# New durations and new ranks for the planner that writes the instruction order of a decoder-layer kernel

## The chip, the cores and the metric

The kernel runs on one core of one Trainium2 chip. The core has a matrix engine (TensorE, PE in the profile; PEld is its weight load), a vector engine (VectorE, DVE), an activation engine (ScalarE, ACT), a general engine (GpSimd, POOL), and SyncE (SP), whose queue issues all the loads and stores here. The engines run side by side, each in the order of its own instruction list, and wait for one another by semaphores. The metric is the device time of one execution in microseconds (us). A profiled execution has a span, from its first instruction to its last; the device time holds the span and a little on both sides of it.

## The reference

The layer takes 1024 tokens of width 1024. In outline:

```python
mod = silu(c) @ w_ada + b_ada                 # shift, scale, gate
h = rms_norm(x, norm_w) * (1 + scale) + shift
u, g_pool, q, k, v, g_attn, qi, ki, wi = split(h @ w_in)
pool_out = pool_mixer(u, w_pool, pool_scale) * silu(g_pool)
q, k = rope(rms_norm(q)), rope(rms_norm(k));  qi, ki = rope(qi), rope(ki)
score = sum_over_8_index_heads(relu(qi . ki) * wi)      # causal
attn  = softmax attention of 8 query heads on 2 key heads,
        only on the 256 keys of the highest score       # per query
y = concat(pool_out, attn * silu(g_attn)) @ w_out
x = x + gate * y
```

`pool_mixer` takes means over the last 2, 4, 8 and 16 tokens minus the token itself, and multiplies them by a matrix per group. Ties in the score go to the earlier key.

## The kernel before

**Stages.** (1) Lead-in: tokens are loaded as rows (`xr`), normed, transposed on PE in pairs of 128 channels (`m<-c,xr`), copied from PSUM to SBUF as `xt` and scaled and shifted to `h`. The w_ada rows (`wa`) are reduced on DVE to scale and shift. (2) Projection: every fp32 product is made from two rounded parts, a high part (`hhi`, `wh`) and the rest (`hlo`, `wl`), in three matmuls: `hhi,wh`, `hhi,wl`, `hlo,wh`. Weights arrive as `ld` and are split by a cast (`wh`) and a subtraction (`wl`). (3) The index scores of the 8 query tiles of 128 tokens, and the search for each row's 256th best score by bisection on the 16-bit halves of the keys: tiles 5 to 7 on ACT (`ajunk<-key,xq`), tiles 2 to 4 on DVE (`junk<-key,xq`), each round followed by small updates (`aq`, `xq`, `yq`). (4) Attention by query tile: scores (`m<-kT,qr`), masked maxima on DVE (`ex<-m,key` or `ex<-m,mask`, and `mx`), exponentials on ACT (`ex<-ex,mx,c`), transposes (`m<-c,ex`), copies (`pw`), products with the values (`m<-pw,vrow`), gating (`mah`, `mal`). Before it, each query half is squared (`st`), split (`qsh`, `qsl`) and summed by head on PE (`m<-qsh,c`, `m<-qsl,c`) for the query norm. After the bisection, a running sum over a tile's ties (`selw<-selw`, a scan) leaves the first ones as the mask. (5) The pooling mixer: window sums on DVE (`nx`, `u`), `m<-u,c` on PE, gating (`gp`), split into `mph` and `mpl`. (6) The output projection in two halves, pooled (`m<-mph,wh` and so on) and attended (`m<-mah,wh`), each finished by a multiply-add (`xo`) and a store.

**What sets the order.** A planner inside the kernel writes all five instruction lists, once, while the kernel is built. Each stage is a set of strands (Python generators such as `token_out`, `queries`, `unit`, `finish`) that yield one operation at a time. `Flow.run` (line 393) asks the next operation of every strand for the time at which it could start by the planner's own clock, adds the strand's rank (`EARLY`; for PE `LAST`, and `SAFE` as a margin on data), and issues the one with the smallest sum. An operation's duration in that clock comes from `Op._cost` (line 169), and the time at which a transfer lands from `Op.issue` (line 224). `Either` (line 284) holds an operation that several engines can do; the engine is the one that would end first, with `FAVOUR` and the engine's backlog added. `KEEP`, `MIX`, `AHEAD`, `WA_AHEAD`, `IK`, `GM` and others limit how many buffers or PSUM banks a strand may take ahead of others, or how far one strand may run ahead of another.

All operations are emitted at one line, L240 of this kernel, so that the profile's rows differ by engine, operation and tile names alone. The lists further below give one engine's instructions in program order; there the scan is written as `SCALAR_TENSOR_TENSOR selw<-selw` and a masked maximum as `ISA ex,mx<-m,key` with an `ISA mx` that reads out its accumulator.

Of the kernel before, what the change touches and what calls it, by code (L numbers as in the profile page):

```python
# [36 lines left out]
ROOM = {"b": 36, "ld": 2, "st": 3, "wh": 4, "wl": 4, "kt": 2, "sg": 2, "selw": 1, "m": 8}  # L37


EARLY = {"main": 0.6, "fill": 0.4, "weights": 0.0, "evac": -1.0, "side": 0.2, "h": -0.2, "mods": -0.2,  # L40
         "select": -0.1, "scores": -0.6, "attend": -1.1, "late": 1.0, "kv": -0.3, "qi": -0.8, "pick": -0.6,
         "mix": -0.33, "rotated": 0.23, "query_loads": 0.21, "exps": -0.11, "score_sums": -1.07,
         "key_value_out": -0.93, "index_queries": -0.86, "norm": -0.46, "gate_loads": -1.94, "token_scales": -3.22,
         "gate_mods": -0.39, "unit": -1.06, "index_scores": -0.91, "lead_loads": 1.12, "out": -1.01,
         "lead_out": -0.62, "weight_loads": 0.77, "key_value_weights": -0.8, "main_line": 1.15, "output_line": 1.13,
         "turns": -1.46, "finish": -1.64, "index_keys": -1.47, "h_block": 0.28, "attention_keys": -0.36,
         "turned": -1.0, "h_blocks": -0.59, "gated": -2.15, "modulations": 0.89, "low": 0.65, "gear": 0.42,
         "attention": -0.86, "maxima": -0.99, "score_relus": -0.67, "gated 7": -1.82, "gated 3": -1.0,
# [5 lines left out]
         "exps 5": -0.25, "key_value_out 4": -3.2, "query_norms": 0.27, "exps 8": -0.52, "key_value_out 5": -1.22,  # L54
# [6 lines left out]
         "key_value_out 6": -2.24, "norm 1": -2.54, "gear 4": -1.05, "products": -1.29, "shift 4": -0.32,  # L61
         "norm 5": -1.64, "low 1": -2.52, "turns 6": -1.25, "gated 6": -2.43, "turns 8": -1.76, "h_block 3": -0.55,
         "shift": 0.73, "gear 8": -1.24, "lead_line": 1.29, "gear 7": -0.86, "index_queries 3": -3.25,
         "index_queries 1": -2.08, "lead_splits": -0.3, "shift 5": -0.34, "first_block": -2.64, "shift 2": -0.27,
         "lead_out 1": -0.38, "shift 8": 1.56, "out 7": -0.3, "unit 3": -1.17, "turns 3": -3.11,
         "key_value_out 1": -2.25, "exps 4": -0.27, "mix 2": -0.2, "exps 2": 0.46, "out 6": -0.73, "gated 8": -2.42,
         "out 5": -2.76, "token_turns": -1.26, "token_out 9": -0.19, "h_half 14": -0.44, "h_half 10": -0.92,
# [6 lines left out]
         "token_tile 4": -0.11, "token_out 10": -1.74, "token_out": -0.47, "token_out 14": -0.77,  # L74
         "token_out 13": -0.78, "token_out 5": -0.25, "h_half 7": -0.24, "token_tile 7": -0.74, "token_tile": -0.23}

SELECT = -0.425
LAST = {"main": 0.12, "fill": -0.081, "scores": 0.035, "attend": -0.104, "evac": -0.027, "qi": 0.257,
        "side": -0.376}

SAFE = {"side": 1.0, "unit": 0, "query_norms": 0.69, "h_block": 0.59, "rotated": 0.48, "query_loads": 0,
        "norm": 0.29, "weight_loads": 0.85, "key_value_out": 0.39, "turned": 0.26, "finish": 0, "index_keys": 0.85,
        "main_line": 0, "output_line": 0, "gate_mods": 1.06, "selection": 0, "low": 0.27, "maxima": 0,
        "attention": 0.44, "lead_out": 0, "score_relus": 0, "lead_loads": 0.28, "score_sums": 0.18, "mix": 0.96,
        "main": 0, "modulations": 0.09, "out": 0.39, "turns": 0.34, "exps": 0, "lead_line": 1.22, "shift": 0,
        "token_scales": 0.08, "index_scores": 0.19, "products": 0.3, "index_queries": 0.34, "attend": 0,
        "weight_splits": 0, "token_turns": 0, "gear": 0, "key_value_weights": 0.29}

COLD = 17.877

# [11 lines left out]

AGE = 0.37

PW_POOL = 0.101
XO_POOL = 0.117
BACK = 0.854
SPAN = 0.119

QK = 1  # L110
IK = 1
FK = 0
PK = 0

GM = 4

MIX = 5
KEEP = 7

FLY = 2  # L120

PV = 5

WA_AHEAD = 1
AHEAD = 4
XN_AHEAD = 2

FAVOUR = {"DVE": 0.245, "ACT": -0.111, "POOL": 0.27}
TABLES = {AF.Silu: 1, AF.Sqrt: 2, AF.Exp: 3}


# [6 lines left out]
class Op:  # L138
# [30 lines left out]
    def _cost(self, aps, kw):  # L169
        size = [a.free_size() for a in aps]  # L170
        n = max(size)
        eng = self.eng
        if eng == "SP":
            return 0.42
        if eng == "PE":
            rate = 2 if self.name == "transpose" else 4 if aps[1].dtype == F32 else 1
            if self.name == "transpose" and aps[1].shape[0] == 64:
                self.mode = "rows"
                return size[0] * 0.000417 + 0.007
            if self.name != "transpose" and min(aps[0].shape[0], aps[1].shape[0]) == 64:  # L180
                self.mode = "rows" if aps[1].shape[0] == 64 else "columns"
                return size[0] * 0.000417 * rate / 2 + 0.007
            return max(0.427 if rate == 4 else 0.109, size[0] * 0.000417 * rate + 0.0135)
        wide = [a for a, k in zip(aps, size) if k == n]
        psum = any(a.space == PSUM for a in wide)
        half = all(mybir.dt.size(a.dtype) == 2 for a in wide)
        if eng == "ACT":
            t = 0.000833 * n + (0.05 if psum else 0.094)
            t += 0.093 * sum(isinstance(kw.get(k), bass.AP) for k in ("scale", "bias", "accum_out"))
            return t  # L190
        if eng == "POOL":
            if self.name == "tensor_tensor":
# [31 lines left out]
    def issue(self, flow):  # L224
        t = self.start(flow)
# [15 lines left out]
        end = t + us  # L241
        flow.clock[self.eng] = end
        if self.eng == "SP":
            flow.dma = max(flow.dma, t + 1.8) + self.kw_bytes() / 4.0e5
            end = flow.dma + (0.35 if self.kw_bytes() > 1e5 else 2.0)
            flow.landed.append(end)
        for a in self.outs:
# [1401 lines left out]
```

## Time and profile before

| what | us |
|---|---|
| device time, median of 3 runs (510.72 to 511.76) | 511.74 |
| span of the profiled execution | 508.7 |
| median minus span | 3.0 |
| PE busy in the span | 481.7 (95%) |
| DVE busy | 420.0 (83%) |
| ACT busy | 380.8 (75%) |
| POOL busy | 148.8 (29%) |

The granted clock of TensorE was 0.995 of full speed on average. For the profiled execution the record gives the span and no device time of its own, so that it is set beside the median of the three runs. In a timeline row the columns are start, duration, engine, line, operation, out<-in tiles, shape and type, how many instructions the row merges, and in brackets the idle time of the engine just before the row and what ended it. By stretches of the span, PE is busy for 17.2 of the first 31.0 us, for 121.75 of the next 122.0, for 84.3 of 87.0 (153 to 240 us), 71.98 of 72.0 (to 312), 79.2 of 83.0 (to 395), 85.7 of 89.0 (to 484), and 21.5 of the last 25.

### The profile page before, as it was taken

Reading aid. Unit: us, or ns where it says so; the run is one execution under the profiler, and the core shown is the slowest. Engines: PE = TensorE matmul, PEld = TensorE weight load, DVE = VectorE, ACT = ScalarE, POOL = GpSimd, SP = SyncE. Lnnn points to the kernel's source line nnn. Section 1 sums busy time; section 2 is a strip of 40 time slices with the busy share of each in tenths; the row PEclk is TensorE's granted clock in tenths of the full one; section 3 lists DMA queues with packets and bytes.
Section 4 is the critical chain, followed back from the end, with each engine's and each line's share of the span. In section 5 each row is a group of like instructions: output and inputs, shape, how many; then the busy total and the mean of one; then the engine's idle time right before and its main releaser. Section 6 shows DMA issues by size and latency. Waiting matters only on the chain.

```text
span 508.7 us, 8547 instructions
## 1 busy us (share of the span) xinstructions
PE 481.7 (95%) x2924; PEld 362.3 (71%) x2924; DVE 420.0 (83%) x914; ACT 380.8 (75%) x877; POOL 148.8 (29%) x182
## 2 busy tenths in 40 slices
PE   1889999999999989999999998999998999999997
PEld 1668999767777867877887776786575558644486
DVE  4987798799789789999999999978889796667453
ACT  3896641687778999999935999899997766669410
POOL 3598053002001133546131235613531232400000
PEclk9999999999999999999999999999998999999999
DMA  8998513011105112111110112685542043521045
GB/s 298 410 407 298 170 41 125 21 36 51 62 22 186 43 42 84 41 42 43 42 52 33 42 43 79 208 273 157 171 128 65 23 124 97 193 63 43 1 150 182
DMA packets 28172, 58.36 MB, mean 115 GB/s; under 512 B 3808, under 2 KB 8416, under 8 KB 28128
## 3 DMA queue, kind: packets, MB, share of 16 engines
q1 hardware_dynamic: 28128, 57.81, 33.9%
q8 instruction: 23, 0.38, 0.3%
q14 instruction: 21, 0.17, 0.1%
HBM read 47.32 MB, written 10.49 MB: 114 GB/s over the span
## 4 chain that ended last, share of the span: by engine, by line
PE 73%; DVE 14%; DMA 6%; ACT 3%; issue 2%; POOL 0%; SPq 0%; DVEq 0%; POOLq 0%
PE m L240 73%; DVE junk L240 4%; DMA wa<-wada 4%; ACT ex L240 3%; DVE ex L240 3%; DVE sw L240 1%; DMA xr<-xR 1%; DVE selw L240 1%; DVE xq L240 1%; DMA ld<-wout 1%; DVE wa L240 1%; DVE mpl L240 0%; DVE qr L240 0%; DVE nx L240 0%; SPq L240 0%
## 5 line engine op out<-in xcount | busy, mean ns | idle before, releaser
L240 PE MATMUL m<-hhi,wh 128*128 128x512 f32 (+1 forms) x320 | 120.8, 400 | 0.6 <-ACT xt L240 0.3
L240 PE MATMUL m<-hhi,wl 128*128 128x512 f32 (+1 forms) x320 | 115.2, 383 | 0.0
L240 PE MATMUL m<-hlo,wh 128*128 128x512 f32 (+1 forms) x320 | 114.9, 382 | 0.0
L240 ACT ACTIVATE ajunk<-key,xq 128x768 bf16<-128x768 uint16 (+2 forms) x93 | 96.4, 1036 | 1.3
L240 PEld LDWEIGHTS m<-hhi,wh 128*128 128x128 f32 x320 | 59.1, 190 | 17.6 <-issue 4.0
L240 DVE TENSOR_SCALAR_CACHE_REDUCE junk<-key,xq 128x384 bf16<-128x384 uint16 (+2 forms) x93 | 69.0, 742 | 2.3 <-DVE xq L240 0.2
L240 POOL TENSOR_TENSOR wl<-ld,wh 128x512 fp32r<-128x512 f32 x42 | 58.2, 1390 | 38.0 <-DVE wh L240 16.7
L240 PEld LDWEIGHTS m<-hhi,wl 128*128 128x128 f32 x320 | 59.2, 190 | 12.2 <-issue 1.7
L240 PEld LDWEIGHTS m<-hlo,wh 128*128 128x128 f32 x320 | 58.7, 189 | 11.6
L240 ACT ACTIVATE ex<-ex,mx,c 128x384 f32<-128x384 f32 (+7 forms) x64 | 54.9, 860 | 6.6 <-DVE mx L240 4.3
L240 DVE SCALAR_TENSOR_TENSOR score<-kt,c,score 128x1024 f32<-128x1024 f32 (+5 forms) x42 | 40.7, 970 | 7.1 <-ACT kt L240 5.0
L240 ACT ACTIVATE kt<-m 128x512 f32<-128x512 f32 (+1 forms) x80 | 37.7, 525 | 11.0 <-DVE score L240 5.2
L240 ACT CAST wh<-ld 128x512 fp32r<-128x512 f32 x31 | 19.3, 624 | 30.5 <-issue 10.6
L240 PE MATMUL m<-kT,qr 64*128 64x512 f32 (+3 forms) x192 | 39.9, 516 | 1.0 <-DVE mx L240 1.0
L240 DVE SCALAR_TENSOR_TENSOR xo<-m,c,xo 128x512 f32<-128x512 f32 (+1 forms) x25 | 18.2, 729 | 24.2 <-PE m L240 16.9
L240 DVE CUSTOM_DVE_ANT_0 ex<-m,key 128x512 f32<-128x512 f32 (+1 forms) x48 | 30.8, 662 | 5.0 <-ACT ex L240 3.6
L240 PE MATMUL m<-pw,vrow 128*64 128x512 f32 x144 | 33.3, 605 | 0.0
L240 PEld LDWEIGHTS m<-kT,qr 64*128 64x128 f32 x192 | 20.4, 190 | 16.1 <-issue 10.6
L240 POOL TENSOR_SCALAR wh<-ld 128x512 fp32r<-128x512 f32 x26 | 17.0, 654 | 48.9 <-PE m L240 28.1
L240 ACT COPY pw<-m 128x512 f32<-128x512 f32 x51 | 26.5, 595 | 5.7 <-PE m L240 5.5
L240 PEld LDWEIGHTS m<-c,ex 64*128 64x128 f32 x576 | 21.0, 138 | 10.9 <-DVE mx L240 3.7
L240 PE MATMUL m<-c,ex 64*128 64x64 f32 x576 | 24.0, 227 | 3.8 <-DVE mx L240 1.8
(199 smaller groups left out, 1029.5 us busy)
## 6 DMA issues: line engine op xcount, KB each, us to landing
wa<-wada SPq DMA_DIRECT2D x24, 512.0 KB, 9.1
ld<-wet SPq DMA_DIRECT2D x16, 512.0 KB, 3.4
ld<-wout SPq DMA_DIRECT2D x24, 256.0 KB, 3.3
xr<-xR SPq DMA_DIRECT2D x8, 512.0 KB, 7.8
xo<-xT SPq DMA_DIRECT2D x16, 256.0 KB, 3.8
y_d<-xo SPq DMA_DIRECT2D x16, 256.0 KB, 2.4
xo<-y_d SPq DMA_DIRECT2D x15, 256.0 KB, 3.1
outT<-xo SPq DMA_DIRECT2D x15, 256.0 KB, 2.5
```

The source lines that it names most:

```text
L240: self.fn(*self.args, **self.kw)
```

## The change

No operation of the layer changes. The planner gets other numbers, and so writes other lists:

- the duration it assumes for a scan becomes twice as long per element, that of a 16-bit two-input operation on DVE half as long;
- a first transfer is assumed to take longer: 3.0e5 bytes per us up to 8 us instead of 4.0e5, and 0.35 us more for a small one;
- nearly all ranks (`EARLY`, `LAST`, `SAFE`) have new values, some strands get one of their own, and the limits, thresholds and engine preferences change.

```diff
-EARLY = {"main": 0.6, "fill": 0.4, "weights": 0.0, "evac": -1.0, "side": 0.2, "h": -0.2, "mods": -0.2,
+EARLY = {"main": 0.05, "fill": 0.4, "weights": 0.0, "evac": -1.0, "side": 0.2, "h": -0.13, "mods": -0.15,
...
-LAST = {"main": 0.12, "fill": -0.081, "scores": 0.035, "attend": -0.104, "evac": -0.027, "qi": 0.257,
-        "side": -0.376}
+LAST = {"main": 0.053, "fill": -0.081, "scores": -0.282, "attend": -0.169, "evac": 0.48, "qi": 0.124, "side": -0.652}
...
-PW_POOL = 0.101
-XO_POOL = 0.117
-BACK = 0.854
-SPAN = 0.119
+PW_POOL = 0.147
+XO_POOL = 0.11
+BACK = 0.835
+SPAN = 0.122
...
-IK = 1
+IK = 3
...
-GM = 4
+GM = 3
-MIX = 5
-KEEP = 7
+MIX = 4
+KEEP = 3
...
-WA_AHEAD = 1
-AHEAD = 4
+WA_AHEAD = 3
+AHEAD = 5
...
-FAVOUR = {"DVE": 0.245, "ACT": -0.111, "POOL": 0.27}
+FAVOUR = {"DVE": 0.278, "ACT": -0.348, "POOL": 0.273}
...
+        if self.name == "tensor_tensor_scan":
+            return 0.00212 * n + 0.069
+        if self.name == "tensor_tensor" and half:
+            return 0.00052 * n + 0.075
...
-            flow.dma = max(flow.dma, t + 1.8) + self.kw_bytes() / 4.0e5
+            flow.dma = max(flow.dma, t + 1.8)
+            flow.dma += self.kw_bytes() / (3.0e5 if flow.dma < 8 else 4.0e5) + (0.0 if self.kw_bytes() > 1e5 else 0.35)
```

The loads stand in the same order as before for the first 41 instructions of SP's list. PE's list has the same stages in the same order; what moves is where the shorter pieces stand between the long rows of projection matmuls, which engine takes some of the shared operations, and the order on DVE, ACT and POOL. Three places:

**The last query norm, on DVE** (`st_2091` before and `st_2100` after are the squares of the last half; the split `qsl` of it stood on POOL before, behind a weight split). Before:

```order
L240 TENSOR_SCALAR junk_2077,cq_330_2076<-key_82,xq_325_2056 128x384
L240 TENSOR_SCALAR junk_2079,cq_330_2076<-key_83,xq_325_2056 128x512
L240 CAST qsh_1964<-st_2091 128x512
L240 TENSOR_SCALAR junk_2084,cq_330_2076<-key_84,xq_325_2056 128x640
L240 TENSOR_SCALAR yq_341_2102<-xq_325_2056 128x3
L240 CAST wh_2092<-ld_1885 128x512
```

Now:

```order
L248 TENSOR_SCALAR junk_2066,cq_328_2065<-key_82,xq_324_2050 128x384
L248 TENSOR_SCALAR junk_2069,cq_328_2065<-key_83,xq_324_2050 128x512
L248 TENSOR_SCALAR junk_2085,cq_328_2065<-key_84,xq_324_2050 128x640
L248 CAST qsh_1970<-st_2100 128x512
L248 TENSOR_TENSOR qsl_1971<-st_2100,qsh_1970 128x512
L248 TENSOR_TENSOR aq_335_2088<-cq_328_2065,kcq_247_1761 128x3
```

The cast now stands behind the whole round of the bisection, and the subtraction follows it on the same engine. On PE the 12 norm matmuls that read these parts come after 1076 matmuls instead of 1064. Of the next group, `m<-u,c`, the first comes after 1226 matmuls instead of 1220, and the next 4 norm matmuls stand right behind it; two products `qr<-qr,cos` of the rotation between the two places have gone from DVE to POOL, and one sum `qr<-qr,sw` from POOL to DVE.

**The scan of the tile of 768 keys, on DVE,** among the masked maxima of the tile of 640 keys (`key_84`). Before:

```order
L240 ISA ex_4339,mx_4161<-m,key_84,mx_4161 128x128
L240 ISA mx_4161 128x1
L240 SCALAR_TENSOR_TENSOR selw_4343<-selw_4343 128x768
L240 ISA ex_4340,mx_4161<-m,key_84 128x512
L240 ISA mx_4161 128x1
L240 TENSOR_TENSOR gt_4160<-gt_4160,m 128x512
L240 ISA ex_4340,mx_4161<-m,key_84,mx_4161 128x128
```

Now:

```order
L248 ISA ex_4245,mx_4178<-m,key_84,mx_4178 128x128
L248 ISA mx_4178 128x1
L248 ISA ex_4227,mx_4051<-m,key_83 128x512
L248 ISA mx_4051 128x1
L248 SCALAR_TENSOR_TENSOR selw_4250<-selw_4250 128x768
L248 ISA ex_4280,mx_4178<-m,key_84 128x512
L248 ISA mx_4178 128x1
L248 TENSOR_TENSOR gt_4050<-gt_4050,m 128x512
```

Before, one head of the tile was still to come behind the scan; now four are. On PE the score matmuls of these heads (`m<-kT,qr`) stand in pairs between groups of 16 transposes and one group of 6 products with the values, before as now.

**The first copies of the lead-in, on ACT** (`xt_187` before and `xt_194` after hold the first two channel blocks). Before:

```order
L240 CAST wh_154<-ld_151 128x512
L240 CAST wh_208<-ld_151 128x512
L240 COPY xt_187<-m 128x8x64
L240 COPY xt_206<-m 128x8x64
L240 COPY xt_187<-m 128x8x64
L240 COPY xt_206<-m 128x8x64
```

Now:

```order
L248 CAST wh_154<-ld_151 128x512
L248 COPY xt_194<-m 128x8x64
L248 CAST wh_218<-ld_151 128x512
L248 COPY xt_214<-m 128x8x64 x2
L248 COPY xt_194<-m 128x8x64
L248 COPY xt_238<-m 128x8x64
```

The second half of the first block is now the fourth copy, where it was the third. Behind it, the `hlo` of the second block has moved from DVE to POOL, where it stands behind two scalings of `xr`.

More of the change, by code (lines that the diff above doesn't have):

```diff
@@ L37 @@
 ROOM = {"b": 36, "ld": 2, "st": 3, "wh": 4, "wl": 4, "kt": 2, "sg": 2, "selw": 1, "m": 8}
-EARLY = {"main": 0.6, "fill": 0.4, "weights": 0.0, "evac": -1.0, "side": 0.2, "h": -0.2, "mods": -0.2,
[L41 to L48, printed above, removed]
[5 rows of a table removed]
-         "exps 5": -0.25, "key_value_out 4": -3.2, "query_norms": 0.27, "exps 8": -0.52, "key_value_out 5": -1.22,
[6 rows of a table removed]
[L61 to L67, printed above, removed]
[6 rows of a table removed]
-         "token_tile 4": -0.11, "token_out 10": -1.74, "token_out": -0.47, "token_out 14": -0.77,
-         "token_out 13": -0.78, "token_out 5": -0.25, "h_half 7": -0.24, "token_tile 7": -0.74, "token_tile": -0.23}
@@ L77 @@
-SELECT = -0.425
-LAST = {"main": 0.12, "fill": -0.081, "scores": 0.035, "attend": -0.104, "evac": -0.027, "qi": 0.257,
-        "side": -0.376}
[L81 to L87, printed above, removed]
+EARLY = {"main": 0.05, "fill": 0.4, "weights": 0.0, "evac": -1.0, "side": 0.2, "h": -0.13, "mods": -0.15,
+         "select": -0.1, "scores": -0.6, "attend": -1.34, "late": 1.0, "kv": -0.68, "qi": -0.53, "pick": -0.6,
+         "mix": -0.01, "rotated": 0.38, "query_loads": -1.36, "exps": -0.18, "score_sums": -1.08,
+         "key_value_out": -1.28, "index_queries": 0.52, "norm": 0.72, "gate_loads": -5.55, "token_scales": -3.22,
+         "gate_mods": -0.39, "unit": -1.2, "index_scores": -3.29, "lead_loads": -1.01, "out": -0.59,
+         "lead_out": 0.68, "weight_loads": 0.13, "key_value_weights": -0.76, "main_line": 3.69, "output_line": 0.46,
+         "turns": 3.89, "finish": -1.64, "index_keys": -1.39, "h_block": -2.15, "attention_keys": -0.43,
+         "turned": -1.0, "h_blocks": -0.03, "gated": -3.43, "modulations": 1.22, "low": 0.65, "gear": 0.43,
+         "attention": -2.89, "maxima": -1.17, "score_relus": -0.67, "gated 7": -2.67, "gated 3": -0.53,
[5 rows of a table added]
+         "key_value_out 7": -2.65, "exps 5": -0.0, "key_value_out 4": -2.92, "query_norms": 1.0, "exps 8": -0.52,
[6 rows of a table added]
+         "shift 6": -0.04, "key_value_out 6": -3.9, "norm 1": -5.07, "gear 4": -1.05, "products": -2.42,
+         "shift 4": -1.67, "norm 5": -2.01, "low 1": -1.0, "turns 6": -7.13, "gated 6": -2.43, "turns 8": -1.76,
+         "h_block 3": -0.55, "shift": 0.73, "gear 8": -1.24, "lead_line": 0.74, "gear 7": -2.86,
+         "index_queries 3": -3.49, "index_queries 1": -2.08, "lead_splits": -0.3, "shift 5": -1.05,
+         "first_block": -2.64, "shift 2": -0.27, "lead_out 1": -0.76, "shift 8": 2.12, "out 7": -0.24,
+         "unit 3": -1.42, "turns 3": -4.24, "key_value_out 1": -2.25, "exps 4": -0.61, "mix 2": -0.2, "exps 2": 0.46,
+         "out 6": -0.48, "gated 8": -2.41, "out 5": -1.53, "token_turns": -1.26, "token_out 9": -0.03,
[6 rows of a table added]
+         "token_tile 8": -0.49, "h_half 13": -0.21, "token_tile 4": -0.11, "token_out 10": -1.62, "token_out": 1.8,
+         "token_out 14": -1.63, "token_out 13": -1.31, "token_out 5": -0.25, "h_half 7": -0.24,
+         "token_tile 7": -0.74, "token_tile": -0.23, "turned 8": -1.3, "weight_splits": 0.08, "maxima 22": -1.87,
[3 rows of a table added]
@@ new lines @@
+SELECT = -0.425
+LAST = {"main": 0.053, "fill": -0.081, "scores": -0.282, "attend": -0.169, "evac": 0.48, "qi": 0.124, "side": -0.652}
+SAFE = {"side": 0.82, "unit": 0, "query_norms": 0.01, "h_block": 0.78, "rotated": 0.48, "query_loads": 0.14,
+        "norm": 0.29, "weight_loads": 0.58, "key_value_out": 0.39, "turned": 0.64, "finish": 0, "index_keys": 0.85,
+        "main_line": 0, "output_line": 0, "gate_mods": 1.57, "selection": 0, "low": 0.24, "maxima": 0,
+        "attention": 0.33, "lead_out": 0, "score_relus": 0, "lead_loads": 0.39, "score_sums": 0, "mix": 0.92,
+        "main": 0, "modulations": 0.17, "out": 0.09, "turns": 0.34, "exps": 0, "lead_line": 1.22, "shift": 0,
+        "token_scales": 0.08, "index_scores": 0.01, "products": 0.3, "index_queries": 0.34, "attend": 0,
+        "weight_splits": 0, "token_turns": 0.13, "gear": 0, "key_value_weights": 0.29, "out_g": 0, "h_half": 0.0,
+        "token_out": 0}
```

37 rows, old and new, of the table EARLY are left out of this document.

## The prediction

> **What bounds the kernel now.** I read the page's busy times and chain first, then PE's waits, and then, for each wait, the timelines around it.
>
> ```profile
> PE 481.7 (95%) x2924; PEld 362.3 (71%) x2924; DVE 420.0 (83%) x914; ACT 380.8 (75%) x877; POOL 148.8 (29%) x182
> PE 73%; DVE 14%; DMA 6%; ACT 3%; issue 2%; POOL 0%; SPq 0%; DVEq 0%; POOLq 0%
> ```
>
> PE is busy for 481.7 of 508.7 us. Since no operation is added or removed, a new order can only work on the 27.0 us that are left, and on what it adds to them. The view of PE's waits says where they are:
>
> ```profile
> PE m L240 <- DVE xr L240: 6.9, 1, 6.9
> PE m L240 <- ACT c L240: 4.9, 1, 4.9
> PE m L240 <- DVE mx L240: 2.8, 5, 1.4
> PE m L240 <- DVE mpl L240: 1.3, 1, 1.3
> PE m L240 <- ACT ex L240: 1.3, 2, 0.8
> PE m L240 <- POOL qsl L240: 0.9, 1, 0.9
> PE m L240 <- DVE u L240: 0.9, 1, 0.9
> PE m L240 <- POOL xr L240: 0.8, 1, 0.8
> PE m L240 <- DVE qsh L240: 0.7, 1, 0.7
> ```
>
> The columns are the sum in us, how often, and the longest. The two first, 11.8 us together, lie before the first real matmul and hang on loads and norms. The others shown sum to 8.7 us, some 1.7% of the span: that is what a better order can win. The end behind the last matmul is no place that the lists change.
>
> **The change part by part.** The duration that the planner assumes costs nothing on the chip; its new ranks and limits matter only through the lists. The order of the first loads is the same as before, so the new transfer times move no arrival there: zero.
>
> *Lead-in.*
>
> ```profile
> 13.74 3.98 PE L240 MATMUL m<-c,xr 64*128 64x64 f32 x64 [6.87 <-DVE xr L240]
> 18.00 1.65 PE L240 MATMUL m<-hhi,wh 128*128 128x512 f32 x3 [0.28 <-DVE hhi L240]
> 19.96 0.80 PE L240 MATMUL m<-hhi,wh 128*128 128x512 f32 x1 [0.31 <-ACT xt L240]
> 26.20 0.71 PE L240 MATMUL m<-c,xr 64*128 64x64 f32 x16 [0.78 <-POOL xr L240]
> 14.45 1.14 ACT L240 CAST wh<-ld 128x512 fp32r<-128x512 f32 x2 [2.43 <-DMA ld<-wq]
> 15.49 2.52 ACT L240 COPY xt<-m 128x512 f32<-128x512 f32 x5
> 17.08 0.87 DVE L240 TENSOR_SCALAR hhi<-xt,c,c 128x512 fp32r<-128x512 f32 x1 [0.50 <-ACT xt L240]
> 18.91 1.27 POOL L240 TENSOR_TENSOR hlo<-xt,hhi 128x512 fp32r<-128x512 f32 x1
> ```
>
> ACT starts when the weights land at 14.45 and then runs without a gap: two casts, 1.04 until the first copy starts, and copies of 0.50 each. The first `hhi` waits for the second half of its `xt`. That copy was ACT's third, after 1.04 + 3 x 0.50 ending near 17.0; it is now the fourth, near 17.55. So `hhi`, and PE's first matmul at 18.00, come some 0.5 later. Against that, PE's 0.31 wait for a copied-out bank at 19.96 should go, because the copies of the other bank come in a row. The second `hlo` now stands on POOL behind two scalings of `xr`, one end of which PE already waited for at 26.20; its 1.27 is partly behind other matmuls, and I charge 0.35. Sum: 0.5 - 0.31 + 0.35, about +0.55. Bounds: 0, if the later copy meets slack, and +1.5, if the copy, 0.5, and most of the `hlo`, 1.0, count in full. Behind it PE has matmuls without a gap from 31 us on, and nothing gives this back.
>
> *Query norms.*
>
> ```profile
> 188.86 0.40 PE L240 MATMUL m<-qsh,c 128*8 128x512 f32 x1 [0.75 <-DVE qsh L240]
> 190.20 0.39 PE L240 MATMUL m<-qsl,c 128*8 128x512 f32 x1 [0.95 <-POOL qsl L240]
> 188.88 1.26 POOL L240 TENSOR_TENSOR qsl<-st,qsh 128x512 fp32r<-128x512 f32 x1 [1.88 <-DVE qsh L240]
> 227.45 0.39 PE L240 MATMUL m<-hlo,wh 128*128 128x512 f32 x1
> 227.68 0.39 PE L240 MATMUL m<-hhi,wh 128*128 128x512 f32 x1
> ```
>
> Two main matmuls start 0.23 apart. The 12 norm matmuls now stand 12 main matmuls later, 12 x 0.227 = 2.72 us. On DVE the cast comes one pass over 640 keys later (0.87, the row at 314.34 below), and the subtraction, before 1.26 on POOL, now follows on DVE, where I estimate 0.65, a little over half of the 1.23 that twice its size takes at 192.04 below. Both are then ready about when the old second wait ended or earlier, with 2.72 less 0.87 of cover: both waits go, -1.70. Bounds: -1.70 and 0.
>
> *The first window sum.*
>
> ```profile
> 226.02 1.12 PE L240 MATMUL m<-u,c 128*128 128x512 f32 x2 [0.90 <-DVE u L240]
> 224.29 1.68 DVE L240 SCALAR_TENSOR_TENSOR u<-nx,u 128x1024 f32<-128x1024 f32 x1
> 192.04 1.23 DVE L240 TENSOR_TENSOR qr<-qr,cos 128x1024 f32<-128x1024 f32 x1
> 230.87 2.40 POOL L240 TENSOR_TENSOR qr<-qr,cos 128x1024 f32<-128x1024 f32 x1 [0.83 <-DVE sw L240]
> ```
>
> PE reaches `m<-u,c` 6 matmuls later, 1.36 us, and that is more than its wait of 0.90. DVE has two products of 1.23 less ahead of `u` and one sum of the same size more. So the wait goes: -0.90. The four norm matmuls right behind it read a split that DVE makes after `u`: I charge +0.2 (0 to 0.5). Bounds together: -0.90 and +0.5.
>
> *Before the output projection.*
>
> ```profile
> 313.36 1.81 PE L240 MATMUL m<-kT,qr 64*128 64x128 f32 x12 [0.53 <-DVE mx L240]
> 315.62 1.25 PE L240 MATMUL m<-kT,qr 64*128 64x256 f32 x6 [0.45 <-DVE mx L240]
> 318.88 0.50 PE L240 MATMUL m<-mpl,wh 128*128 128x512 f32 x1 [1.35 <-DVE mpl L240]
> 314.34 0.87 DVE L240 TENSOR_SCALAR_CACHE_REDUCE junk<-key,xq 128x640 bf16<-128x640 uint16 x1
> 316.25 2.58 DVE L240 TENSOR_TENSOR mpl<-gp,mph 128x1024 fp32r<-128x1024 f32 x1
> 315.38 2.37 POOL L240 TENSOR_TENSOR mpl<-gp,mph 128x1024 fp32r<-128x1024 f32 x1
> ```
>
> 2.33 us of waits. DVE's bisection pass of 0.87 no longer stands among the maxima; a cast that was on ACT has come to DVE ahead of them. `mpl` is a two-input operation, and at 316.25 it took 2.58 where the same size took 1.23 at 192.04: POOL's own two-input operation ran until 317.75, and DVE's took 1.1 from there. POOL's two `mpl` now stand back to back, so this overlap stays. I take -0.6, near the 0.87 that leaves the run of maxima; bounds -1.5 and 0. The Trainium skill's GPSIMD Engine Reference (Specifications) says that GpSimd shares its SBUF interfaces with VectorE, in contention with VectorE instructions that read two SBUF inputs; the row of 2.58 agrees. By that rule alone this term would be 0 and the sum 0.6 less of a gain.
>
> *The scan.*
>
> ```profile
> 390.36 0.72 PE L240 MATMUL m<-c,ex 64*128 64x64 f32 x16 [1.35 <-DVE mx L240]
> 387.58 2.13 DVE L240 TENSOR_TENSOR_SCAN selw<-selw 128x768 uint16<-128x768 bf16 x1
> ```
>
> PE waits here for a PSUM bank that DVE's maxima have yet to read, and DVE is in the scan from 387.58 to 389.7. With the scan earlier, 2.1 us of DVE work leave the end of the tile; a wait can open at the new place, where four heads are pending. I take -1.0 (bounds -1.35 and +0.8, the scan's 2.13 less the 1.35 that it exposed here).
>
> *The last tile.*
>
> ```profile
> 470.05 0.46 PE L240 MATMUL m<-c,ex 64*128 64x64 f32 x8 [0.54 <-ACT ex L240]
> 471.27 1.27 PE L240 MATMUL m<-c,ex 64*128 64x64 f32 x34 [0.76 <-ACT ex L240]
> 458.08 3.03 ACT L240 COPY pw<-m 128x512 f32<-128x512 f32 x6 [2.05 <-PE m L240]
> ```
>
> ACT ran eight exponentials of 1024 behind these six copies. Now four stand ahead of the copies, and PE issues the tile's last scores before its long row of transposes. Half of 1.30 goes: -0.6 (bounds -1.3 and 0).
>
> *New waits.* A new order has its own small misses. Before, the 5 waits for `mx` took 2.8. I charge one of the size of the longest, +1.3, with bounds 0 and 2.8.
>
> Sum: 0.55 - 1.70 - 0.90 + 0.2 - 0.6 - 1.0 - 0.6 + 1.3 = -2.75. Against the span that is 508.7 - 2.75 = 505.95, and with the 3.0 that the median of the runs lies above the span, 509.0. (The profiled execution has no device time of its own on record.)
>
> **The rivals.**
>
> ```profile
> 31.00:153.00 122.00, 121.75 (x774) 100.69 (x774) 103.44 (x140) 80.75 (x176) 32.35 (x25) 1.00 0.31 110
> ```
>
> *All named waits go and none come* (chance 0.10): 0.55 - 1.70 - 0.90 - 1.5 - 1.35 - 1.3 = -6.2, so 505.5. For it: in the projection stretch above (the columns are the window, its length, and the busy time of PE, PEld, DVE, ACT and POOL) PE has 121.75 of 122.0 us, so a list without gaps exists there. Against: in the attention stretch PE has little long work left to lay over.
>
> *No change, by DVE and POOL in each other's way* (0.19). Two `qr<-qr,cos` of 2.40 now run on POOL while DVE has two-input work. If they hold DVE up as `mpl` shows (1.3 each), `u` loses what it gained, the waits at 313 to 319 stay, and the scan's and last tile's gains are eaten by new waits of their size: 0.55 - 1.70 + 0.2 + 1.3 = +0.35, and with half of the scan's gain -0.15: 511.6. For it: DVE is 83% busy. Against: the query norms' wait has 1.9 us of cover.
>
> *Slower, by the scans* (0.16). The three scans of 768, 896 and 1024 keys take some 2.1 us each. If each now stands with score banks unread and PE has less than 0.8 of other work, each opens a wait like the one at 390.36. Three of 1.35 instead of one: +2.7. With the lead-in at its upper bound, +1.5, the norms -1.70, nothing at 313 to 319, and no gain at `u`, the sum is +2.5: 514.2. It decides from the point at which PE's work between two pairs of scores is shorter than the scan. For it: more heads are pending behind the first scan than before. Against: the planner now gives a scan a duration near the real one (2.13 us for 768 keys), and so sees the wait that it makes.
>
> *That the change doesn't do what it says:* for the first transfers this is so, the loads stand as before, and it is in the forecast at zero.
>
> **How the numbers follow.** The forecast of 509.0 has 0.55. With the first rival, faster by over 0.2% (below 510.7, about the least that a measurement here can tell) has 0.65; the second is within 0.2% (0.19); the third, slower (0.16). The likeliest case's own range, its new waits between 0 and 2.8 and the lead-in between 0 and 1.5, is 507.2 to 511.4. To hold 8 in 10 the range has to take in most of the second rival and the lower half of the third, and part of the first: 506.2 to 512.9.
>
> **What would show it.** Right: no wait for `qsl` or `qsh` near 190 us and none for `u` near 226; PE's wait in the transposes near 390 below 0.4; the waits for `ex` near 470 below 0.7 in sum; the first main matmul between 18.3 and 18.6. Wrong: PE's idle time before some 32 us up by more than 1.5; new waits of PE for `mx` with a scan on DVE; `u` still late with `qr<-qr,cos` on POOL ahead of it. If PE's busy time itself moves by more than 1 us, the sum was made on the wrong base.

## The result

The changed kernel took 517.4 us (median of 4 executions, 516.4 to 518.5); the kernel before took 511.3 beside it (510.7 to 511.8). The ratio is 1.0114, with a 95% interval of 1.0089 to 1.0139: slower by about 6 us, where 509.0, 2.7 us below the 511.74 known then, was forecast, and outside the range. The profiled execution of the changed kernel took 517.2 with a span of 515.5, so 1.7 us lie around the span, and the same holds for executions of the kernel before (511.49 with a span of 509.8). The 3.0 that the prediction put there was too much: the profiled execution of before, with its span of 508.7, must have taken about 510.4 by this, less than the three executions (510.72 to 511.76) that the prediction set it beside.

The page of the changed kernel, busy times and chain:

```profile
PE 486.1 (94%) x2924; PEld 366.5 (71%) x2924; DVE 418.9 (81%) x906; ACT 385.5 (75%) x887; POOL 151.6 (29%) x180
PE 57%; DVE 18%; ACT 15%; issue 5%; DMA 2%; POOL 2%; SPq 1%; DVEq 0%; POOLq 0%
```

PE has the same 2924 matmuls and is busy 4.4 us longer (481.7 before). Its idle time went from 27.0 to 29.4. So of the 6.8 us of span, only 2.4 are waiting; 4.4 are matmuls that run slower. Where, the view by stretches of time shows. First the kernel before, then the changed one; the columns are the window, its length, the busy time of PE, PEld, DVE, ACT and POOL with the number of instructions, and then the granted TensorE clock, 1.00 being full:

```profile
150.00:240.00 90.00, 87.09 (x392) 68.33 (x389) 83.92 (x182) 84.92 (x211) 31.84 (x37) 1.00 0.20 68
240.00:300.00 60.00, 60.00 (x258) 48.29 (x257) 57.82 (x136) 46.23 (x109) 15.39 (x30) 1.00 0.13 39
300.00:345.00 45.00, 42.66 (x196) 33.09 (x197) 40.24 (x126) 42.90 (x117) 19.99 (x22) 1.00 0.53 166
```

```profile
150.00:240.00 90.00, 90.00 (x406) 71.58 (x406) 86.00 (x187) 86.53 (x213) 39.88 (x41) 1.00 0.21 74
240.00:300.00 60.00, 55.97 (x225) 43.40 (x225) 57.09 (x130) 46.89 (x110) 17.02 (x30) 0.94 0.11 36
300.00:345.00 45.00, 42.91 (x187) 33.60 (x186) 36.33 (x103) 36.75 (x98) 20.80 (x22) 0.92 0.45 144
292.00:296.00 4.00, 3.01 (x5) 1.79 (x6) 3.43 (x9) 3.97 (x12) 0.23 (x1) 0.54 0.02 7
296.00:300.00 4.00, 4.00 (x10) 2.44 (x10) 3.79 (x10) 1.83 (x5) 2.21 (x4) 0.60 0.00 0
320.00:324.00 4.00, 3.91 (x11) 2.25 (x10) 4.00 (x15) 1.93 (x4) 1.31 (x2) 0.50 0.59 185
```

Up to 240 us the change does what was forecast: 406 matmuls where there were 392, and no idle time. Between 240 and 300 it loses all of that and more, 225 matmuls for 258, and the clock falls below 1. In four microseconds from 296, PE is busy without a gap and does 10 matmuls; at full clock it does 17 to 20. The record of the granted clock in the trace holds three stretches at exactly half before the last matmul: 6.83 us from 292.4, 6.83 from 319.7, and 3.41 from 394.8. The kernel before has one, 3.41 from 391.4.

What starts each is a wait of PE. Rows of PE's timeline in the changed kernel (start, length, operation, and in brackets the idle time before it and what ended it), with two main matmuls behind the first wait:

```profile
292.99 2.07 PE L248 MATMUL m<-u,c 128*128 128x512 f32 x2 [3.77 <-DVE u L248]
296.14 0.63 PE L248 MATMUL m<-hhi,wh 128*128 128x512 f32 x1
296.57 0.63 PE L248 MATMUL m<-hhi,wl 128*128 128x512 f32 x1
318.06 3.16 PE L248 MATMUL m<-kT,qr 64*128 64x128 f32 x18 [2.01 <-DVE mx L248]
393.23 0.46 PE L248 MATMUL m<-c,ex 64*128 64x64 f32 x8 [0.80 <-ACT ex L248]
395.25 1.12 PE L248 MATMUL m<-c,st 128*128 128x128 f32 x4 [0.95 <-ACT st L248]
466.13 0.27 PE L248 MATMUL m<-c,ex 64*128 64x64 f32 x1 [1.19 <-ACT pw L248]
```

At half clock the main matmuls start 0.43 apart; at full clock it was 0.23. The two large waits are for DVE. The first is for `u` of the third group of the pooling mixer, a place where PE did not wait before; the second is at the first scores. In the kernel before, DVE had this `u` ready 2.1 us ahead of PE:

```profile
286.17 1.55 DVE L240 SCALAR_TENSOR_TENSOR u<-nx,u 128x1024 f32<-128x1024 f32 x1
289.87 1.02 PE L240 MATMUL m<-u,c 128*128 128x512 f32 x2
```

The timelines of DVE and of POOL around the two waits in the changed kernel:

```profile
284.54 0.92 DVE L248 TENSOR_TENSOR aq<-cq,kcq 128x3 f32<-128x3 f32 x1
285.56 1.28 DVE L248 SCALAR_TENSOR_TENSOR xq<-aq,yq 128x3 f32<-128x3 f32 x1
291.71 1.22 DVE L248 SCALAR_TENSOR_TENSOR u<-nx,u 128x1024 f32<-128x1024 f32 x1
315.49 2.31 DVE L248 TENSOR_TENSOR aq<-cq,kcq 128x3 f32<-128x3 f32 x1
317.72 0.28 DVE L248 CUSTOM_DVE_ANT_0 ex<-m,mask 128x128 f32<-128x128 f32 x1
```

```profile
283.06 2.37 POOL L248 TENSOR_TENSOR nx<-nx 128x1016 f32<-128x1016 f32 x1 [1.63 <-DVE nx L248]
285.53 1.28 POOL L248 TENSOR_TENSOR wl<-ld,wh 128x512 fp32r<-128x512 f32 x1
315.04 5.04 POOL L248 TENSOR_TENSOR mpl<-gp,mph 128x1024 fp32r<-128x1024 f32 x2 [0.63 <-DVE mph L248]
```

Two things make DVE late. On DVE, this `u` stands behind 21 rounds of the bisection of the rows of tiles 2 to 4, where it stood behind 19; PE reaches its reader later too, but only by 2.8 us of matmuls (counted in the order, at 0.23 us for 512 columns), and two rounds are 6 to 8.8 (3.0 to 4.4 each by the starts of `aq` in the kernel before). PE came to the reader at 289.22, 0.65 us sooner than before, and `u` was done at 292.94, 5.2 later. And small operations of the bisection on three columns, `aq` and `xq`, which take 0.16 alone, are held until POOL's operation with two inputs ends: the `aq` at 284.54 runs to 285.46, where the `nx` of 2.37 ends at 285.43; the one at 315.49 takes 2.31 beside POOL's two `mpl`. The groups of all 31, from the lists of groups before and after (busy time in us and mean ns of one, then DVE's idle time before them):

```profile
L240 DVE TENSOR_TENSOR aq<-cq,kcq 128x3 f32<-128x3 f32 x31 | 8.1, 261 | 0.5
```

```profile
L248 DVE TENSOR_TENSOR aq<-cq,kcq 128x3 f32<-128x3 f32 x31 | 13.8, 445 | 0.5
```

How far PE's work had fallen behind, from first and last matmuls of a kind (before, after): the first `m<-wkh,hhi` 59.80 and 60.09, the last `m<-hhi,wh` 310.70 and 313.91, the first `m<-mph,wh` 316.80 and 321.14, the first `m<-mah,wh` 400.72 and 406.84, the last matmul 505.25 and 511.96.

### The profile page after: what moved, and what is told of

Read it like the earlier page. It is cut to its first block, busy times and chain, and to the rows that moved or that the text cites. A ratio compares the mean times of both kernels' runs of the same rounds, so it can differ in the third digit from the quotient of the medians.

```text
span 515.5 us, 8552 instructions
## 1 busy us (share of the span) xinstructions
PE 486.1 (94%) x2924; PEld 366.5 (71%) x2924; DVE 418.9 (81%) x906; ACT 385.5 (75%) x887; POOL 151.6 (29%) x180
## 4 chain that ended last, share of the span: by engine, by line
PE 57%; DVE 18%; ACT 15%; issue 5%; DMA 2%; POOL 2%; SPq 1%; DVEq 0%; POOLq 0%
PE m L248 57%; ACT ajunk L248 6%; DVE junk L248 5%; DVE ex L248 3%; ACT ex L248 2%; DMA ld<-wq 2%; DVE nx L248 2%; DVE selw L248 2%; ACT aq L248 1%; ACT xq L248 1%; DVE aq L248 1%; ACT st L248 1%; SPq L248 1%; ACT qr L248 1%; DVE xq L248 1%
## 5 line engine op out<-in xcount | busy, mean ns | idle before, releaser
L248 ACT ACTIVATE ex<-ex,mx,c 128x256 f32<-128x256 f32 (+7 forms) x64 | 55.0, 861 | 9.3 <-DVE mx L248 9.3
L248 ACT COPY pw<-m 128x512 f32<-128x512 f32 x56 | 29.1, 603 | 7.2 <-PE m L248 6.1
L248 PEld LDWEIGHTS m<-kT,qr 64*128 64x128 f32 x192 | 20.6, 189 | 17.1 <-issue 9.6
L248 PE MATMUL m<-c,ex 64*128 64x64 f32 x576 | 25.3, 232 | 3.6 <-ACT pw L248 1.7
```

The lines of the kernel that those rows point to most:

```text
L248: self.fn(*self.args, **self.kw)
```

## The experiments

Two theories were set against each other. **A**: a few badly placed operations (`u`, one `aq`) make the waits, and putting these few right takes the waits and the half clock away. **B**: between 280 and 350 the whole of DVE's work is too late for PE, with the bisection's rounds too far ahead, and the wait moves to whatever is due next. In both, a wait costs more than its length because TensorE runs at half clock behind it. Except for those with the durations or the ranks alone, each kernel issues the recorded order of its base with the named rows moved, so that nothing else in the planner's order shifts. Diffs of an order show rows of one engine.

**`u` of the third group earlier.** On DVE:

```diff
 SCALAR_TENSOR_TENSOR xq<-aq,yq 128x3
+TENSOR_TENSOR nx<-nx,c 128x16
+SCALAR_TENSOR_TENSOR u<-nx,u 128x1024
 TENSOR_SCALAR junk,cq<-key,xq 128x384
...
-TENSOR_TENSOR nx<-nx,c 128x16
...
-SCALAR_TENSOR_TENSOR u<-nx,u 128x1024
```

> The changed kernel, replayed with its own lists, with one difference: on DVE the two last steps of the third window sum (nx times the counts, and u) stand before the bisection round that they stood behind. In the changed kernel TensorE waited 3.77 us for this u at 292.99, and its granted clock was 0.5 for the 6.8 us that followed. Theory A, the wait is a local misplacement that costs its length and the half-speed stretch: u is ready when TensorE comes, the wait goes, and so do some 3.1 us that the next matmuls lost at half speed; 517.4 - 6.9 = 510.5. Theory B, DVE's whole stream up to the masked maxima at 317.7 is the bound: TensorE is early at the scores instead and waits there for mx 2.0 + 5 to 7 us; only one of two half-speed episodes and some 1.5 us of DVE's own idle time go: 512.5 to 514.

**One `aq` ahead of the two `mph` casts,** so that POOL's `mpl` does not hold it:

```diff
+TENSOR_TENSOR aq<-cq,kcq 128x3
 CAST mph<-gp 128x1024
 CAST mph<-gp 128x1024
-TENSOR_TENSOR aq<-cq,kcq 128x3
```

> The changed kernel, replayed, with one difference: on DVE the small comparison aq (128x3) stands before the two casts mph, not behind them. In the changed kernel it took 2.31 us at 315.49, where 0.16 is usual, because GpSimd had begun its two-input mpl at 315.04; the masked maxima stood behind it, TensorE waited 2.01 us for their banks at 318.06 and ran at half clock for 6.8 us after. Theory A (an operation with two SBUF inputs on DVE is held until GpSimd's two-input operation ends, and the wait sits on the path): aq takes 0.16, the maxima start some 2.1 us earlier, TensorE's wait is under 0.5, and 2.0 + 2.7 at half clock go: 512.7. Rival (the maxima would be late anyway, because the casts and mpl hold DVE): no more than 1 us goes, 516.4 to 517.4.

**Both:**

> Both moves together. If both waits are local (theory A twice): 517.4 - 6.9 - 4.7 = 505.8, faster than the kernel before. If DVE's stream is the bound (theory B): TensorE reaches the scores some 7 us earlier, DVE reaches the maxima only 2 to 3.5 us earlier, and a wait of 4 to 5 us stands there: 510 to 512.

**Matmuls without use in the wait,** 16 of 512 columns into the bank that the late `m<-u,c` is about to fill (PE does this extra work):

```diff
-                yield mm(ps, wp_sb[:, g, :], u[:, c], True, True)
+                fill = [mm(ps, hhi[0][:, 0:P], hhi[0][:, 0:512], True, True) for _ in range(16)]
+                fill = fill if len(mixed_u) == 4 else []
+                yield Group(fill + [mm(ps, wp_sb[:, g, :], u[:, c], True, True)])
+                mixed_u.append(g)
```

> The changed kernel, replayed, with 16 matmuls of 128x512 that compute nothing used, put on TensorE right before the late m<-u,c, into the bank that this matmul then overwrites: 16 x 0.227 = 3.6 us, which fill the wait of 3.77. The wait for u is as long, but TensorE is not idle in it. If the granted clock falls because of the idle time, it stays at 1.0 here, and the half-speed loss of 3.1 us goes; under theory A of the first run the time is then 514.3. Under theory B TensorE is only earlier at the scores and waits there some 3 us longer: 516.5 to 517.4, or less if that wait has no half-speed stretch of its own.

Against 510.5 for the kernel before beside them, the four took 514.7 (ratio 1.0085, 1.0053 to 1.0118), 515.4 (1.0109, 1.0063 to 1.0156), 515.0 (1.0110, 1.0064 to 1.0156) and 516.4 (1.0120, 1.0089 to 1.0150). By time none can be told from the changed kernel, and the first three medians fall outside all that was expected; the fourth, 516.4, is at the lower end of B's 516.5 to 517.4. The traces tell more. With `u` of the third group early, its wait is gone, and by PE's timeline the next two places wait:

```profile
303.17 2.08 PE L372 MATMUL m<-u,c 128*128 128x512 f32 x2 [3.77 <-DVE u L372]
315.34 3.40 PE L372 MATMUL m<-kT,qr 64*128 64x256 f32 x16 [2.00 <-DVE mx L372]
```

The 3.77 is now at `u` of the fourth group. With `aq` early it took 0.16, and the wait at the scores fell from 2.01 to 1.45, but one of 2.16 for `mpl` opened behind it. With both, the sum that A expected (505.8) did not come, nor B's 510 to 512: the waits were 3.76 at the fourth `u` and 2.18 at `mpl`. A falls: each wait that is taken away comes back at the next place. B's prices were too low as well. PE's timeline with the extra matmuls:

```profile
292.86 1.13 PE L372 MATMUL m<-u,c 128*128 128x512 f32 x2 [0.15 <-DVE u L372]
317.36 3.78 PE L372 MATMUL m<-kT,qr 64*128 64x128 f32 x18 [3.47 <-DVE mx L372]
```

Nothing at half clock follows the first row (the clock stays full until 316.6). So the half clock there comes with PE's idle time, and not with the late `u` itself. But PE, now earlier, waits 3.47 at the scores, and half clock follows there for 6.83 us.

**The converse, in the kernel before:** the last two steps of `u` of the third group go behind ten more steps of the bisection.

```diff
-TENSOR_TENSOR nx<-nx,c 128x16
 TENSOR_SCALAR junk,cq<-key,xq 128x640
-SCALAR_TENSOR_TENSOR u<-nx,u 128x1024
...
 TENSOR_SCALAR junk,cq<-key,xq 128x512
+TENSOR_TENSOR nx<-nx,c 128x16
+SCALAR_TENSOR_TENSOR u<-nx,u 128x1024
```

> The converse, in the kernel before: on DVE the last two steps of u of group 3 stand behind one bisection round and two thirds more (ten steps, about 5.5 us of DVE), everything else in the same order. u was done 2.1 us ahead of PE, so PE waits for it 3 to 4 us. If TensorE at half clock after a wait is part of the price (as the changed kernel's rows say), a stretch of 3.4 or 6.8 us at half clock follows at about 293 and costs another 1.7 to 3.4: span 508.7 + 5 to 7 = 514 to 516, time 516 to 518. If the wait is the whole price: no such stretch, span 512 to 512.7, time 514.5 to 515.5. If what follows had slack enough to swallow it: 511 to 512.

It took 514.7 against 510.1 (1.0073, 1.0044 to 1.0101), with a span of 514.0. PE's timeline, and then the windows behind the wait:

```profile
294.15 2.07 PE L363 MATMUL m<-u,c 128*128 128x512 f32 x2 [3.05 <-DVE u L363]
```

```profile
292.00:296.00 4.00, 1.85 (x3) 0.83 (x3) 2.06 (x4) 1.61 (x4) 0.00 (x0) 0.68 0.00 0
296.00:300.00 4.00, 4.00 (x10) 2.64 (x8) 0.75 (x1) 1.13 (x5) 0.00 (x0) 0.50 0.00 0
```

One late `u` in the good kernel reproduces the picture: a wait of 3.05 and then 6.83 us at half clock. DVE and ACT stand still there as well (0.75 and 1.13 of 4.00 us): they are next to read banks that PE fills at half speed. The first `m<-kT,qr` came 7.3 us later than before, of which 1.0 was there from the lead-in on; 3.05 + half of 6.83 = 6.5 is close to the other 6.3. So at the scores the wait of 3.05 us has cost about double its length. By the end some of that had been made up (last matmul +4.3 beside the lead-in): the wait of 1.35, at 390 before, stands at 397 here, but no half clock followed it this time. The time, 514.7, came where the wait alone was expected to bring it (514.5 to 515.5), and not at 516 to 518. Nor was the price the same each time: the profiled execution was the slowest of the four (515.7), and by their mean clock, 0.997, two others (513.8 and 513.9) lost only some 1.5 us in all to half clock.

**The bisection later.** On DVE and POOL, its steps from the 19th round on take the place of the step one round behind, and the lag is given back towards the end. Then the same with two rounds, where one ACT operation that needs the bisection's result (`sg`) goes later too. The diff is that of one round, on DVE.

```diff
-TENSOR_SCALAR junk,cq<-key,xq 128x384
-TENSOR_SCALAR junk,cq<-key,xq 128x512
 CAST wh<-ld 128x512
-TENSOR_SCALAR junk,cq<-key,xq 128x640
 TENSOR_TENSOR nx<-nx,c 128x16
-TENSOR_TENSOR aq<-cq,kcq 128x3
-SCALAR_TENSOR_TENSOR xq<-aq,yq 128x3
 TENSOR_SCALAR junk,cq<-key,xq 128x384
-TENSOR_SCALAR junk,cq<-key,xq 128x512
 SCALAR_TENSOR_TENSOR u<-nx,u 128x1024
+TENSOR_SCALAR junk,cq<-key,xq 128x512
...
```

> The changed kernel with the bisection of the rows of tiles 2 to 4 (its steps on DVE and POOL) one round later from its 19th round on: each of its steps takes the place in the order that the step one round behind it had, over seven rounds, and the lag is given back over the last rounds. All else on DVE (u of groups 3 and 4, gp, the mph casts, the maxima) so comes some 3 us earlier among them; PE, ACT and SP issue in the same order. Theory B (DVE's whole stream is late between 280 and 320, and TensorE at half clock after the waits adds to it): the 4.0 us of waits for u and the 2.0 us for mx mostly go, with them at least one of the two stretches at half clock of 6.8 us; 515.5 - 5 - 3.4 = about 507 of span, 509 to 511 of time. Rival (the bisection itself is what is due next): its end, 346.7 in the changed kernel, comes out later and the wait moves to the scores behind it at 346 to 360; 514 to 517.

> As the kernel with the bisection one round later (513.6), but two rounds later from the 19th on, given back by the end; u of groups 3 and 4, gp, the mph casts and the maxima so come another 3 us earlier on DVE. There the waits left at the scores were 2.20 us for mx and 0.86 for mpl, with 10.2 us at half clock behind them. Theory B: these go, 513.7 - 2.2 - 0.9 - 3.4 to 5.1 = 505.5 to 507.2 of span, 507 to 510 of time, not slower than the kernel before. Rival (the bisection's own end becomes due): a wait of 2 us or more for mx at the scores of tile 3 near 345 to 352, 511 to 514.

One round later: 513.6 against 510.1 (1.0067, 1.0042 to 1.0092), between the two ranges that were expected. The last `m<-hhi,wh` is at 307.8, 6.1 us ahead of the changed kernel, and 2.9 ahead of the kernel before. What is left, by PE's timeline:

```profile
289.84 1.13 PE L372 MATMUL m<-u,c 128*128 128x512 f32 x2 [0.48 <-DVE u L372]
312.14 3.39 PE L372 MATMUL m<-kT,qr 64*128 64x128 f32 x18 [2.20 <-DVE mx L372]
317.54 0.80 PE L372 MATMUL m<-mpl,wh 128*128 128x512 f32 x1 [0.86 <-DVE mpl L372]
```

Both waits for `u` and the half clock behind them are gone, as B says; those at the scores are not, and 10.24 us at half clock follow them. Two rounds later came out slower again, 518.2 against 510.6 (1.0172, 1.0118 to 1.0226), above the rival's 511 to 514 as well, but at the place that the rival named: the bisection's own end is now due, at the first scores of tile 3 in PE's timeline.

```profile
347.85 0.91 PE L372 MATMUL m<-kT,qr 64*128 64x384 f32 x2 [1.40 <-DVE xo L372]
350.81 1.65 PE L372 MATMUL m<-kT,qr 64*128 64x384 f32 x2 [2.05 <-DVE mx L372]
```

**One window sum back from POOL to DVE:** the `nx` of 128x1016 of the third group.

> The changed kernel with one operation of the first window sum of group 3, the tensor_tensor nx of 128x1016, back on DVE, as in the kernel before; everything else in the same order. On POOL it took 2.37 us from 283.06 and DVE's aq (0.92 for 0.16) and xq (1.28 for 0.16) of 284 to 287 were held; on DVE it takes 1.2 us itself. Theory (DVE's two-input operations are held while POOL's run, so the move to POOL won DVE nothing): DVE reaches u 0.5 to 1 us earlier, the wait of 3.77 us becomes 2.8 to 3.3, time 516 to 517. If the move had relieved DVE: the wait grows to about 5, time 518 to 519.

It took 514.9 against 510.6; the interval, 1.0059 to 1.0152, holds the changed kernel's 1.0114, so the time decides nothing. In the trace `aq` and `xq` after 284 are back at 0.16, and the wait for `u` is 3.39 (3.77 before this edit; 2.8 to 3.3 was expected). Putting that sum on POOL had won DVE nothing, but this is a tenth of the wait, not its cause.

**Durations alone, ranks alone.** The kernel before with the new durations only, and the changed kernel with the old durations only:

> The kernel before with only the scheduler's new durations (running sum, 16-bit pairs, first transfers); ranks and rules stay as they were. In the orders it writes, u of group 3 stands on DVE behind 20 bisection rounds at PE's old place (19 before, 21 in the changed kernel, where PE's place is 2.8 us later), and u of group 4 behind 24 (23 before). If the durations are harmless and the ranks carry the loss: 510 to 512. If any order written for other ranks is late at u: a wait of 1 to 3 us there, 512 to 515.

> The changed kernel with the old durations: only ranks and rules are new. u of group 3 stands behind 20 rounds at the changed kernel's place on PE, u of group 4 behind 23, POOL has the nx of 1016 columns and one more of 1023. If the ranks carry the loss as such: 515 to 518. If the loss is the lateness of DVE's stream (theory B), u of group 3 is one round (3 to 4 us) earlier than in the changed kernel and its wait is gone: 510 to 514.

Both are far slower than either whole: 528.3 (1.0336, 1.0306 to 1.0366) and 526.3 (1.0306, 1.0275 to 1.0336); no expected range held. With the durations alone 7.3 of 18.6 us are lost in the lead-in: the same 328 matmuls stand ahead of the first `m<-wkh,hhi`, which starts at 67.13 (59.80 before), after waits near 56 to 62 us and half clock from 28.3 and 62.4. The first `m<-kT,qr` is 9.9 us later than before, the first `m<-mah,wh` 16.3, the last matmul 18.6. With the ranks alone the longest wait for `u` is 1.10, as B would have it, and PE is ahead of the kernel before by 2.8 us at the first `m<-mah,wh` (397.96), and loses it behind that, as PE's timeline shows:

```profile
480.19 0.28 PE L244 MATMUL m<-c,ex 64*128 64x64 f32 x2 [2.20 <-ACT ex L244]
482.64 0.46 PE L244 MATMUL m<-c,ex 64*128 64x64 f32 x8 [2.17 <-ACT ex L244]
```

In this kernel durations and ranks work only together, and the change cannot be split into a harmless and a harmful part. What makes the two halves so slow in detail stays open.

**The head of one and the tail of the other:** the order of the ranks alone up to the first `m<-mah,wh`, the changed kernel's from there.

> The order that the new ranks give with the old durations (the run of 526.3) up to the first matmul of the attended output projection, and the changed kernel's order from there. The first began that projection at 397.96, 2.8 us ahead of the kernel before and 8.9 ahead of the changed kernel, and lost 18 us behind it in waits for ex; the changed kernel needs 105.1 us from there to its last matmul. If head and tail add up: 398.0 + 105.1 + 3.5 = 506.6 of span, 508 to 510.5 of time, faster than the kernel before. If the head's lead is borrowed (work on ACT and DVE put off into the tail): waits for ex return, 513 to 525.

It took 515.0 against 510.6 (1.0087, 1.0056 to 1.0118); the profiled execution was the quickest of its ten, 511.8, with one stretch at half clock, and the slowest took 518.4. By their mean clocks, the loss to half clock (one less the mean clock, times the span) was 2.0 us in the two at 511.8 and 512.1, and 10.3 in the one at 518.4. The order is the same in all ten. Its waits of 2.02 for `mx` at 312.9 and of 1.11 at 382 stand where they were in the head's own kernel. No wait for `ex` came back, so the rival's reason is not what made it slow, though the time lies in the rival's range; in the profiled execution the head ended 2.5 us later than in its own kernel (400.43) and the tail took 106.2.

**Three repairs of DVE's order together:** the bisection one round later, the `nx` back on DVE, and the round that stood ahead of the `mph` casts moved behind the sixteen maxima. The last of these:

```diff
 SCALAR_TENSOR_TENSOR xq<-aq,yq 128x3
-TENSOR_SCALAR junk,cq<-key,xq 128x384
-TENSOR_SCALAR junk,cq<-key,xq 128x512
-TENSOR_SCALAR junk,cq<-key,xq 128x640
 CAST mph<-gp 128x1024
 CAST mph<-gp 128x1024
-TENSOR_TENSOR aq<-cq,kcq 128x3
...
+TENSOR_SCALAR junk,cq<-key,xq 128x384
+TENSOR_SCALAR junk,cq<-key,xq 128x512
 TENSOR_SCALAR junk,cq<-key,xq 128x640
+TENSOR_TENSOR aq<-cq,kcq 128x3
```

> The changed kernel with three repairs of DVE's order: the bisection one round late from the 19th on (513.6 alone), nx of 128x1016 back on DVE (514.9 alone), and the round that stood ahead of the two mph casts moved behind the sixteen maxima, so that these start when PE's first scores are there. Theory B adds up what is left in the profile with the round late: 513.7 - 2.2 (mx) - 0.9 (mpl) - 3.4 to 5.1 (half clock behind them) + up to 2 (the bisection ends later, scores of tile 3 near 350) = 505.5 to 509.2 of span, 507 to 511 of time. If every place won is lost at the next due one, as with two rounds late: 512 to 516, again a stretch at half clock behind 310 or 346.

It took 509.2 (507.7 to 509.4 over 12 executions) against 510.3: a ratio of 0.9974, with an interval of 0.9959 to 0.9988, faster than both kernels. The span is 505.9. Its page's busy times, and PE's timeline at the scores:

```profile
PE 480.6 (95%) x2924; PEld 363.3 (72%) x2924; DVE 416.5 (82%) x907; ACT 385.3 (76%) x887; POOL 152.4 (30%) x179
```

```profile
311.43 1.36 PE L372 MATMUL m<-kT,qr 64*128 64x128 f32 x12 [1.24 <-ACT st L372]
314.48 0.50 PE L372 MATMUL m<-mpl,wh 128*128 128x512 f32 x1 [1.03 <-DVE mpl L372]
```

PE's order, ACT's and the loads' are those of the changed kernel; only DVE's and POOL's lists differ. The wait for `u` is 0.16, the one at the scores 1.24, and no half clock follows either; PE is busy 5.5 us less than in the changed kernel with the same matmuls. The profiled execution was the quickest of the twelve, but the mean clock of all twelve (0.989 to 0.997) lies above that of every execution of the changed kernel (0.979 to 0.985). This shows the cause: the loss was DVE's order (with POOL's) between 280 and 350 us, and the clock that its waits cost. With these repairs the new order is 1.1 us faster than the kernel before, inside the 507 to 511 expected here, and still less than the prediction's gain.

## Why the prediction was wrong

**The lead-in** (+0.55) came out as forecast in the profile, the first main matmul at 18.60 and +0.29 at the first `m<-wkh,hhi`, but that is luck as far as the runs show. The nine profiles with this lead-in have that matmul between 17.37 and 18.70 and the first `m<-wkh,hhi` between 58.99 and 60.24; the two with the old one have 18.00 and 18.14, and 59.80 and 60.76. Executions differ by more than the term. **The first transfers** at zero: right in the whole change, though with the durations alone the lead-in came out 7.3 us longer.

**The query norms** (-1.70) and **the first window sum** (-0.90): right; no wait stands near 190 or 226. But these gains were spent at the third `u`: PE came there 0.65 us sooner than before, with 2.8 us more of matmuls done, and DVE was not ready.

**Before the output projection** (-0.6): wrong. The waits went only from 2.33 to 2.01, and in one piece, and half clock came behind them. The prediction had named both causes, the cast that came to DVE ahead of the maxima and POOL's two `mpl` back to back, and took from them only that the overlap stays. An `aq` stood between the casts and the maxima and took 2.31.

**The scan** (-1.0): the wait of 1.35 for `mx` went, but 0.80, 0.34 and 0.95 for `ex` and `st` came within 3 us of it, and the stretch at half clock stayed: 0.74 more of waits, near the upper bound. **The last tile** (-0.6): the 1.30 for `ex` went, 1.19 and 0.21 for `pw` came, and nothing was gained.

**New waits** (+1.3, bounds 0 to 2.8) is the term that failed first. Its size was taken from the waits for `mx` that the kernel before had, and the places looked at were those where PE waited before. The largest new wait, 3.77, is at a `u` that had been ready 2.1 us early. Its cover was never counted: two more rounds of the bisection ahead of it on DVE, 6 to 8.8 us on an engine that has 57.8 of 60.0 us of work there, against that lead of 2.1 and 2.8 us more of matmuls on PE. The difference, 1.1 to 3.9, could be read from the orders and the rows of the kernel before. The two orders of DVE had this to give at the third `u`; the prediction compared them at the first only.

**The base** failed next: "a new order can only work on the 27.0 us that are left". It also works on the 481.7, through the clock: 17.1 us at half clock before the last matmul instead of 3.4, and 4.4 us more of busy time with the same matmuls. The prediction had this as the sign that its sum stood on the wrong base, and gave it no chance.

**The rivals.** DVE and POOL in each other's way is in the rows, the 31 `aq` take 5.7 us more, but it is the smaller part: with the `nx` back on DVE the wait only fell from 3.77 to 3.39, and 511.6 was far too low. The slower rival had the sign and the wrong cause: the waits for `mx` near 316 stand behind casts and a held `aq`, not behind a scan.

## What to carry to other kernels

When an order is changed, compare at every place where one engine reads another's result how far the maker is ahead, in work on both engines, and not only at the places that waited before; a bound engine's gain is spent at the first place where the next engine has no lead. A wait of TensorE of some 3 us can cost about twice its length, as it did here in one execution, and another execution may pay little more than the length; so judge an order by waits that are long or come close together, not by their sum alone, and by several executions. Planner durations and ranks belonged together here: half of the pair was worse than either whole.

## What the hardware showed that was not expected

**Half clock after short waits.** In the fourteen profiles of this case the record of the granted clock changes on a grid of 3.41 us. Counting from 36 us on how long PE was idle in each window of the grid that ran at full clock: with 1.9 us or more, half clock followed in 16 of 16; with 1.3 to 1.9, in 17 of 27; with 1.2 to 1.3, in 1 of 4; with 0.1 to 1.2, in 1 of 157. A stretch lasts one window, or two or three where PE is idle again inside it, and there less is enough: of the windows at half clock, the 11 with 0.64 us or more of idle time were all followed by another one, and 2 of the 37 with 0.5 or less. The Trainium skill's "TensorE: Matmul & The Clock Gate" (Part 1, "What's actually happening") gives the window as 3413 ns, free-running, and half clock after an idle window; window and grid agree with the trace, but here 1.3 to 2 us of idle time in a window were often enough.

**The same wait, with and without it.** The grid starts elsewhere in each execution. The waits of 1.19 and 0.21 at the last tile stand in ten profiles with this tail or a like one; half clock followed where both fell into one window (six profiles, 1.40 idle), and did not in the other four, where 0.91 to 1.22 us did. The wait of some 2 us for `mx` at the first scores shows it too: with the ranks alone it fell into one window and half clock followed; in the kernel of head and tail it was split into 0.66 and 1.36, and none followed. This goes with a good part of the spread between executions of one order: of the 50 executions of the kernel before whose clock is on record, the 8 whose mean clock is full took 508.4 to 510.3, and the 10 that lost 4.5 us or more to half clock 511.5 to 512.9. One of these ten, at 512.9, does not fit: its mean clock of 0.948 would be a loss of 26.6 us.

**A small operation held by a large one.** An operation of DVE on 128x3 with two inputs, 0.16 alone, took up to 2.36 us in the changed kernel beside POOL's `tensor_tensor`, until that ended. It fits the rule on two SBUF inputs that the prediction cites; what was not expected is that the smallest operation pays as much as a large one.
